# Reading the skewed bias tiles of a banded attention straight from their table, with a row step of minus one element

## The chip, the cores and the metric

The kernel runs on one core of one Trainium2 chip. The metric is the device time of one execution in microseconds (us); the median of the runs counts. A core has a matrix engine (TensorE, PE in the profile), three engines for elementwise work (VectorE or DVE, ScalarE or ACT, GpSimd or POOL) and a queue engine (SyncE, SP) that issues nearly all transfers here. The transfers run on 16 DMA engines.

## The reference, cut to what matters

One encoder layer over 1,024 tokens of width 1,024. After a first norm, two attentions run side by side: a dense one with low-rank queries and keys (8 heads, with rotary positions) and a banded one (16 heads, each token sees 128 to either side, with a bias by distance and a sink). Their gated sum goes through an output product, then comes a feed-forward part with a convolution, and a last norm. The change touches the bias of the banded attention:

```python
rel = c - WINDOW - a                     # column minus row, in a band of 128 query rows
in_band = jnp.abs(rel) <= WINDOW
bias = rel_bias[t5_bucket(rel)]          # one value per distance and head
s = einsum('bqhgd,bkhd->bhgqk', q_blk, k_blk) * scale + bias
s = jnp.where(valid, s, -1e30)           # then a softmax with the sink as one more column
```

The bias depends on the distance alone, so a row of the bias band is the row above it, moved by one element.

## The kernel before, in words

Products are made in three passes of a high and a low part, so TensorE has most of the work. The program is written stage by stage. A scheduler fixes each engine's order from estimated times, except for TensorE in the stages that matter here, whose order is written out by hand (`manual_schedule`). Every engine runs its own list in order, and an instruction that waits holds up all that stand behind it. This is so for SP too: its list of transfers is one queue.

**First stage** (lines 184 to 412). For each of eight row tiles i of 128 tokens: norm (`scaled`, `normed`), eight transposes into `pt`, a split into `ht_h` and `ht_l` (line 130), and the latent product into `pj` (line 262, 24 matmuls). `tile_step(i)` then writes the scaled latents to DRAM (`lat_d`, line 392) and keeps the rotary key `kr` (line 391). In between TensorE makes, per head h, the product of two up-projections: three transposes into `pw` (line 321), a copy by ScalarE into `wt` (line 323), the product `pm` (line 329), and a copy by VectorE into `wqk` (line 331), which goes to DRAM. `pj`, `pw` and `pm` share four PSUM buffers. The rotary tables are made by `rope_tables` (line 335): positions are loaded into `pos_i` (line 337; 1,024 elements of 4 bytes), cast to `pos_f` (line 339), and a chain of some fifteen VectorE steps over `ang` and `kk` leads to a sine and a cosine on ScalarE (lines 359, 360). `pos_i` uses one of the two buffers of `wt`.

**The bias.** Lines 282 to 291 make the small table `tc_d` in DRAM: 16 heads by 512 distances (`TW`), 32 KB. Lines 293 to 296 copy it out eight times, once for each pair t of heads, with 64 copies (`HQ`) of each head's row: `tb_d[t]` has 128 rows of 2 KB. Step `s1(t, 0)` of the banded stage (line 626) loads the bias tile `bt`, 128 rows by 320 columns (`BAND`), in two loads of 64 rows each (line 631). In each the row step is `TW - 1` elements, so that every row starts one element earlier in its copy.

**What follows.** The values of the banded attention and the rotated queries (lines 526 to 600) run after the first stage. `prep(i)` reads the latents back (`ltile`, line 520), transposes them, splits them into `lth` and `ltl` (two buffers each), and writes these to DRAM (`lt_d`, lines 574 and 575); the product `pjr` uses `lth`. Then `steps()` runs the banded attention, eight pairs t of eight steps n, with `bt` in two buffers; weights `raw` (line 103) are loaded, cast by ScalarE into `whi` (line 107), and reduced by GpSimd to `wlo` (line 110). The dense attention, the output product and the feed-forward part come after it.

Of the kernel before, what the change touches and what calls it, by code (L numbers as in the profile page):

```python
# [11 lines left out]
F32 = mybir.dt.float32  # L12
# [8 lines left out]
P = 128  # L21
# [3 lines left out]
KD = D // P  # L25
# [14 lines left out]
HQ = P // 2  # L40
BAND = HQ + 2 * WINDOW
# [6 lines left out]
TW = 512  # L48
# [28 lines left out]
def encoder_layer(ctx, tc, x, positions, norm1_g, w_in, q_a_norm_g, w_q_b, kv_a_norm_g, w_kv_b,  # L77
                  rel_bias, sinks, w_out, norm2_g, w_up, conv_w, conv_b, w_down, final_norm_g,
                  onehot, freq, out):
    nc = tc.nc  # L80
# [5 lines left out]
    dp = ctx.enter_context(tc.tile_pool(name="dp", bufs=1, space=bass.MemoryType.DRAM))  # L86
# [3 lines left out]
    mx_d = [dp.tile([P, 4, 2, KD, P], F32, name=f"mx_d{j}") for j in range(2)]  # L90
    mx_l = dp.tile([P, 4, 2, P], F32, name="mx_l")
    tc_d = dp.tile([H_B, TW], F32, name="tc_d")
    tb_d = {}
    lt_d = [dp.tile([P, 4, S], F32, name=f"lt_d{j}") for j in range(2)]
    qr_d = [dp.tile([P, H_A, 512], F32, name=f"qr_d{j}") for j in range(2)]
    lat_d = dp.tile([NT, P, Q_LORA + KV_LORA], F32, name="lat_d")
# [35 lines left out]
    def three(ps, terms):  # L132
        n = len(terms)
        for i, (a, b) in enumerate(terms):
            nc.tensor.matmul(ps, a, b, start=(i == 0), stop=(i == n - 1))  # L135
# [15 lines left out]
    def row(pool, src, n, name):  # L151
        t = pool.tile([P, n], F32, name=name)
        nc.sync.dma_start(t, bass.AP(src.tensor, src.offset, [[0, P], [1, n]]))
        return t
# [26 lines left out]
        ht_h.append(big([P, KD, 512], f"ht_h{j}"))  # L181
        ht_l.append(big([P, KD, 512], f"ht_l{j}"))

    # first norm, latents of the dense branch, tables
    with ExitStack() as p0:
        rp = p0.enter_context(tc.tile_pool(name="rp", bufs=1))
        ps = p0.enter_context(tc.tile_pool(name="ps0", bufs=1, space=PSUM))
# [66 lines left out]
        def latents(i, ks=range(KD)):  # L254
            if i not in pjs:
                pjs[i] = ps.tile([P, 512], F32, tag="pj", bufs=4, name="pj")
            tok = slice(i % 4 * P, (i % 4 + 1) * P)
            for k in ks:
                wh, wlo = wl[k // 2][0][:, k % 2, :], wl[k // 2][1][:, k % 2, :]
                th, tl = ht_h[i // 4][:, k, tok], ht_l[i // 4][:, k, tok]  # L260
                for j, (a, b) in enumerate(((th, wh), (th, wlo), (tl, wh))):
                    nc.tensor.matmul(pjs[i][:, :LAT], a, b, start=(k + j == 0), stop=(k == KD - 1 and j == 2))

        with tc.manual_schedule(engines={getattr(mybir.EngineType, e) for e in FIRST}):
# [13 lines left out]
            wl_lo(3, nc.vector)  # L278
            parted(1)
            latents(0, range(4, KD))  # L280
        # relative bias by distance, masked outside the window, then one copy per query row
        rb = rp.tile([33, H_B], F32, name="rb")
        nc.vector.memset(rb[32:33, :], 1.0)
        nc.sync.dma_start(rb[0:32, :], rel_bias)
# [5 lines left out]
        nc.vector.tensor_copy(tb, tp[0:H_B, :])  # L290
        nc.sync.dma_start(tc_d, tb)

        for t in range(KD):
            if t < KD:
                tb_d[t] = dp.tile([2, HQ, TW], F32, name=f"tb_d{t}")
                nc.sync.dma_start(tb_d[t], tc_d[2 * t:2 * t + 2, None, :].broadcast_to([2, HQ, TW]))

        srow = row(rp, sinks, H_B, "srow")
        for j in range(2):
            rows = slice(j * HQ, (j + 1) * HQ)  # L300
# [3 lines left out]
        qg = row(rp, q_a_norm_g, Q_LORA, "qg")  # L304
        kg = row(rp, kv_a_norm_g, KV_LORA, "kg")

        # per head, the product of the query and key up-projections
        wqk_v = wqk_d.rearrange("k p h c -> p k h c")
        wqn = []
        wts = {}  # L310
# [20 lines left out]
            nc.vector.tensor_copy(wqk_, pm[:, :2])  # L331
            nc.sync.dma_start(wqk_v[:, :, h, :], wqk_)

        # token tables of the rotary embedding
        def rope_tables():
            pos_i = rp.tile([P, NT], I32, tag="wt", bufs=2, padded_shape=[P, 3 * P], name="pos_i")
            nc.sync.dma_start(pos_i, positions.rearrange("(t p) -> p t", p=P))
# [63 lines left out]
        for i in range(HELD, NT):  # L401
            tile_step(i)

        # taps and bias of the convolution, one column per block of channels
        cwr = rp.tile([2 * NF, 4, P], F32, name="cwr")
        for j in range(4):
            src = conv_w[j] if j < 3 else conv_b[0]
# [23 lines left out]
        three(pj, terms)  # L431
        split(pair[0], pair[1], pj)

    # window branch and gates
    with ExitStack() as pa:
        ap_ = pa.enter_context(tc.tile_pool(name="ap_", bufs=1, reuse_waits="tile"))
        ps = pa.enter_context(tc.tile_pool(name="psA", bufs=1, space=PSUM, reuse_waits="tile"))
# [73 lines left out]
                        nc.sync.dma_start(ga_d[t][:, h_ * 512:(h_ + 1) * 512], gts.pop((t, "a", h_)))  # L511
            return [project(w, hf, post) for hf in range(2)]

        # values, token-major, high and low parts side by side
        ltiles = []

        def load_lt(n):
# [108 lines left out]
        def s1(t, n):  # L626
            g = t // 2
            if n == 0:
                bt = bts[t] = ap_.tile([P, BAND], F32, tag="bt", bufs=2, name="bt")
                for j in range(2):  # L630
                    nc.sync.dma_start(bt[j * HQ:(j + 1) * HQ],
                                      bass.AP(tb_d[t].tensor, tb_d[t].offset + j * HQ * TW + P - 1,
                                              [[TW - 1, HQ], [1, BAND]]))
            bt = bts[t]
            flat = sts[t, n] = ap_.tile([P, 2 * BAND + 2], F32, tag="st", bufs=3, name="st")
            nm = cp.tile([P, 2], F32, tag="nm", bufs=4, name="nm")
            sm = cp.tile([P, 2], F32, tag="sm", bufs=4, name="sm")
            spans = []
            for e in range(2):
                q0 = (2 * n + e) * HQ  # L640
                k0, k1 = max(q0 - WINDOW, 0), min(q0 + HQ + WINDOW, S)
                a = 1 + e * BAND + k0 - q0 + WINDOW
                spans.append((k0, k1, a, a + k1 - k0, k0 - q0 + WINDOW))
            if n == 0:
                nc.gpsimd.memset(flat[:, 1 + BAND:1 + BAND + HQ], 0.0)
            if n == NT - 1:
                nc.gpsimd.memset(flat[:, 1 + BAND - HQ:1 + BAND], 0.0)
            ends = [spans[0][2] - 1, spans[1][3]]
            nc.gpsimd.tensor_copy(flat[:, ends[0]:ends[1] + 1:ends[1] - ends[0]],
                                  nsink[:, t:t + 1].broadcast_to([P, 2]))  # L650
            for e in range(2):
                k0, k1, a, b, c0 = spans[e]
                m = 2 * n + e
                sc = ps.tile([P, 512], F32, tag="sc", bufs=2, name="sc")
                q_ = qss[t, m // 8][:, m % 8].rearrange("p j q -> p (j q)")
                three(sc[:, :k1 - k0], [(q_, kws[g][0][:, k0:k1]), (q_, kws[g][1][:, k0:k1])])
                nc.vector.tensor_tensor_reduce(
                    out=flat[:, a:b], in0=sc[:, :k1 - k0], in1=bt[:, c0:c0 + k1 - k0], scale=-1.0,
                    scalar=nsink[:, t:t + 1], op0=ALU.add, op1=ALU.min, accum_out=nm[:, e:e + 1])
                ex = flat[:, a - 1:b] if e == 0 else flat[:, a:b + 1]  # L660
                nc.scalar.activation(ex, ex, AF.Exp, bias=nm[:, e:e + 1], scale=-1.0, accum_out=sm[:, e:e + 1])
            ri = cp.tile([P, 2], F32, tag="ri", bufs=4, name="ri")
            nc.vector.reciprocal(ri, sm)  # L663
            if 0 < n < NT - 1:
                pn = flat[:, 1:1 + 2 * BAND].rearrange("p (e c) -> p e c", e=2)
                nc.gpsimd.tensor_tensor(pn, pn, ri[:, :, None].broadcast_to([P, 2, BAND]), op=ALU.mult)  # L666
            else:
                for e in range(2):
                    _, _, a, b, _ = spans[e]
                    nc.gpsimd.tensor_tensor(flat[:, a:b], flat[:, a:b], ri[:, e:e + 1].broadcast_to([P, b - a]),  # L670
                                            op=ALU.mult)
# [47 lines left out]
            next(rot, None)  # L719
        drain(rot)  # L720

        # transposed weights; the halves of a key tile that a row tile doesn't see stay zero
        pths = [[ap_.tile([P, 6, P], F32R, tag=t, bufs=2, name=t) for t in ("pth", "ptl")] for _ in range(2)]
        for w in pths[0] + pths[1]:
            nc.gpsimd.memset(f32(w[HQ:, 0]), 0.0)
# [4 lines left out]
        q0_ = queries(0)  # L730
        drain(q0_[0])
        s1(0, 0)
        drain(q0_[1])
        def steps():
            for t in range(KD):
# [13 lines left out]
                for n in range(NT):  # L749
                    for stage in range(3):  # L750
                        if stage == 0:
                            if n + 1 < NT:
                                s1(t, n + 1)
                            elif t + 1 < KD:
                                s1(t + 1, 0)
                        elif stage == 1:
                            s2(t, n)
                        elif n > 0:
                            s3(t, n - 1)
                        elif t > 0:  # L760
                            s3(t - 1, NT - 1)
                        pos += 1
                        while done < math.ceil(total * pos / 24):
                            next(chain_, None)
                            done += 1
                    if n == NT - 1:
                        drain(chain_)
                    if (t, n) == (KD - 1, ABS):
                        wqk[0] = absorbing(0)
                    yield t, n  # L770
# [7 lines left out]

    ck.close()

    # dense branch
    c1 = ExitStack()
    cc1 = c1.enter_context(tc.tile_pool(name="cc1", bufs=1, reuse_waits="tile"))

# [44 lines left out]
    with ExitStack() as pb:  # L829
# [110 lines left out]
        for i in range(ni):  # L940
# [12 lines left out]
            if i in (ni - 16, ni - 14, ni - 12, ni - 7):  # L953
                j = len(wos[0])
# [13 lines left out]
        if EARLY > 2:  # L968
            out_early(2)

    # output projection, residual, second norm; the blocks of the up product's second operand
    hq = c0.enter_context(tc.tile_pool(name="hq", bufs=1, side="right", reuse_waits="tile"))
    hs = [big([P, 2, 4, 512], f"hs{j}") for j in range(4)]
    B11, B21, B22, T1, T2, T3, T4 = range(7)
# [143 lines left out]
    first = [0, 0, 1] + [0] * 5 + [1] * 6  # L1118
# [129 lines left out]
        ready += [next(todo) for _ in range(5)]  # L1248
    c1.close()

    # up projection by seven block products (Strassen's scheme in Winograd's form), convolution and gate
    with ExitStack() as pd:
        dd = pd.enter_context(tc.tile_pool(name="dd", bufs=1, reuse_waits="tile"))
        dpool["dd"] = dd
# [55 lines left out]
    c3.close()  # L1310
    c0.close()

    # down projection by the same scheme, final norm
    with ExitStack() as pe_:
        for name in ("op", "x2", "part", "raw"):
            dpool[name] = pe_.enter_context(tc.tile_pool(name="d_" + name, bufs=1, reuse_waits="tile"))
# [13 lines left out]
        halves = (slice(0, 512), slice(512, D))  # L1330
# [24 lines left out]
        for gi, group in enumerate(groups):  # L1355
# [3 lines left out]
            for bank, phase, outs in phases:  # L1359
# [8 lines left out]
                for j, tp in turns_:  # L1368
                    if up_ and j == 0:
                        banks[bank, tp] = ps.tile([P, 512], F32, tag=bank, bufs=4, name="b" + bank)  # L1370
                    a, w = opers[j]
# [57 lines left out]
```

## Time and profile before

| what | us |
|---|---|
| three runs | 1697.89, 1698.56, 1701.55 |
| median | 1698.56 |
| span of the profiled execution (first to last instruction) | 1695.9 |
| TensorE busy in that span | 1597.8 |
| VectorE, GpSimd, ScalarE busy | 1075.1, 973.2, 900.7 |

The page gives the span of the profiled execution and no other time of it; the span is 2.7 us under the median of the runs. Times inside the execution are counted from the span's start. A row of the timeline has the start, the length, the engine, the line, the operation with its output and inputs, how many instructions are merged, and in brackets the idle time of the engine ahead of it with what ended it. "SPq" rows are the queue's own instructions that issue a transfer; their length is the time until the issue was done, not until the data landed.

### The profile page before, as it was taken

To read this page: it belongs to the slowest core of one execution; us is meant where nothing else is said; L and a number is where in the kernel's file an instruction comes from. 1 tells how busy PE (TensorE), PEld (TensorE's weight loads), DVE (VectorE), ACT (ScalarE), POOL (GpSimd) and SP (SyncE) were. 2 spreads that over 40 slices of the span, in tenths; PEclk is the share of its full clock that TensorE was granted. 3 is DMA by queue.
4 is the path that set the end of the run, shared out by engine and by line. 5 is a ranking of instruction groups with operands and counts; after the bars stand their busy time and mean duration, and the time that the engine had idled before them with its cause. 6 is when DMAs were issued, how large, how long until landed. Compare 5 with 4: busy or idle time off the path is not lost. (4 is left out here: it accounts for less than half of the span.)

```text
span 1695.9 us, 21962 instructions
## 1 busy us (share of the span) xinstructions
PE 1597.8 (94%) x7714; PEld 1318.9 (78%) x7714; DVE 1075.1 (63%) x1781; ACT 900.7 (53%) x1684; POOL 973.2 (57%) x755
## 2 busy tenths in 40 slices
PE   8299999999999999999999998999999999699998
PEld 7288788878887788888887877888888888477786
DVE  7157556556556566666653386665566665999997
ACT  6124787767787565555551264444445444343345
POOL 3002344333333375656561078888989985888884
PEclk9699999999999999999999999999999999799999
DMA  7346122111210721213125943222222222714202
GB/s 252 93 142 196 38 60 60 56 59 48 63 48 21 259 100 52 67 54 134 51 87 166 317 144 97 77 88 75 87 70 84 83 87 84 301 50 136 103 11 99
DMA packets 150102, 173.81 MB, mean 102 GB/s; under 512 B 10711, under 2 KB 111879, under 8 KB 149992
## 3 DMA queue, kind: packets, MB, share of 16 engines
q1 hardware_dynamic: 147368, 163.83, 29.4%
q0 software_dynamic: 2624, 8.59, 1.5%
q8 instruction: 61, 1.00, 0.2%
q14 instruction: 49, 0.40, 0.1%
HBM read 124.64 MB, written 49.84 MB: 103 GB/s over the span
## 5 line engine op out<-in xcount | busy, mean ns | idle before, releaser
L1112 PE MATMUL bx<-hs,op 128*128 128x512 f32 x1056 | 260.2, 398 | 5.0 <-ACT cv L1299 3.4
L1112 PEld LDWEIGHTS bx<-hs,op 128*128 128x128 f32 x1056 | 200.5, 190 | 53.0 <-ACT cv L1299 3.9
L1112 PE MATMUL byz<-hs,op 128*128 128x512 f32 x792 | 196.1, 395 | 1.6 <-ACT k L1271 1.0
L860 POOL TENSOR_TENSOR p<-p,rib 128x1024 f32<-128x1024 f32 x64 | 123.2, 1936 | 111.3 <-DVE rib L859 74.3
L1112 PEld LDWEIGHTS byz<-hs,op 128*128 128x128 f32 x792 | 149.4, 189 | 36.9 <-ACT k L1271 1.4
L445 PE MATMUL pj<-ht_h,whi 128*128 128x512 f32 x416 | 169.5, 407 | 0.0
L445 PE MATMUL pj<-ht_h,wlo 128*128 128x512 f32 x416 | 164.5, 396 | 0.0
L445 PE MATMUL pj<-ht_l,whi 128*128 128x512 f32 x416 | 164.4, 395 | 0.0
L1375 PE MATMUL bx<-op,op 128*128 128x512 f32 x528 | 134.0, 413 | 19.2 <-DVE x L789 14.1
L110 POOL TENSOR_TENSOR wlo<-raw,whi 128x512 fp32r<-128x512 f32 x64 | 82.7, 1320 | 111.4 <-ACT whi L107 111.0
L786 POOL TENSOR_TENSOR op<-s,op 128x512 fp32r<-128x512 f32 x80 | 139.6, 1749 | 8.6 <-ACT op L984 8.6
L1375 PEld LDWEIGHTS bx<-op,op 128*128 128x128 f32 x528 | 105.6, 201 | 44.9 <-DVE x L789 15.4
L666 POOL TENSOR_TENSOR st<-st,ri 128x640 f32<-128x640 f32 x48 | 60.1, 1252 | 120.8 <-DVE ri L663 120.6
L129 ACT CAST pT<-pt 128x512 fp32r<-128x512 f32 x128 | 73.8, 589 | 93.7 <-PE pt L874 93.5
L130 DVE TENSOR_TENSOR pT<-pt,pT 128x512 fp32r<-128x512 f32 x128 | 86.9, 683 | 53.1 <-ACT pT L129 53.1
L130 DVE TENSOR_TENSOR ptl<-ptw,pth 64x128 fp32r<-64x128 f32 (+2 forms) x176 | 74.3, 422 | 68.8 <-ACT pth L129 66.7
L786 POOL TENSOR_TENSOR op<-wu,op 128x512 fp32r<-128x512 f32 x64 | 96.2, 1516 | 30.0 <-ACT op L984 29.7
L852 DVE TENSOR_REDUCE nmb<-sc 128x1 f32<-128x1024 f32 x64 | 78.3, 1224 | 33.9 <-PE sc L135 33.5
L1375 PE MATMUL by<-op,op 128*128 128x512 f32 x396 | 95.5, 395 | 4.2 <-DVE op L786 3.8
L1020 ACT CAST op<-p 128x512 fp32r<-128x512 f32 x88 | 50.6, 617 | 83.1 <-PE bx L1375 54.6
L135 PE MATMUL po<-pT,ct 128*128 128x512 f32 x384 | 94.6, 395 | 0.0
L135 PE MATMUL sc<-lt_h,q 128*128 128x512 f32 x224 | 93.6, 418 | 0.0
(294 smaller groups left out, 3964.8 us busy)
## 6 DMA issues: line engine op xcount, KB each, us to landing
wu<-in_w_up_dram SPq DMA_DIRECT2D x44, 512.0 KB
raw<-in_w_in_dram SPq DMA_DIRECT2D x28, 512.0 KB
act_d<-t SPq DMA_DIRECT2D x22, 512.0 KB
ra<-act_d SPq DMA_DIRECT2D x22, 512.0 KB
rw<-in_w_down_dram SPq DMA_DIRECT2D x22, 512.0 KB
mh<-mx_d SPq DMA_DIRECT2D x16, 512.0 KB
mh<-mx_d SPq DMA_DIRECT2D x12, 448.0 KB
xt<-in_x_dram SPq DMA_DIRECT2D x8, 512.0 KB
```

The source lines that it names most:

```text
L110: nc.gpsimd.tensor_tensor(lo[:, q], raw[:, q], f32(hi[:, q]), op=ALU.subtract)
L129: nc.scalar.copy(hi, src)
L130: nc.vector.tensor_tensor(lo, src, f32(hi), op=ALU.subtract)
L135: nc.tensor.matmul(ps, a, b, start=(i == 0), stop=(i == n - 1))
L445: nc.tensor.matmul(pj, a[:, k, :], b[:, k], start=(k + j == 0), stop=(k == KD - 1 and j == 2))
L666: nc.gpsimd.tensor_tensor(pn, pn, ri[:, :, None].broadcast_to([P, 2, BAND]), op=ALU.mult)
L786: eng.tensor_tensor(dst, a, b, op=ALU.subtract)
L852: nc.vector.tensor_reduce(nm, sc, axis=AX.X, op=ALU.max, negate=True)
L860: nc.gpsimd.tensor_tensor(pe, pe, ri.broadcast_to([P, S]), op=ALU.mult)
L1020: nc.scalar.copy(t[:, 0], src)
L1112: nc.tensor.matmul(bank, a[:, i, k], hs[c][:, j, k], start=(start and n == 0), stop=(n == 11), skip_group_check=not start)
L1375: nc.tensor.matmul(banks[bank, tp], l_, r_, start=(up_ and j + n == 0), stop=(j == len(group) - 1 and n == 2), skip_group_check=not up_)
```

## The change

`tb_d` and its eight copies are gone. `bt` is loaded by one transfer of 128 rows whose source is `tc_d` itself: two heads, 64 rows per head with a step of minus one element, 320 elements each.

```diff
     tc_d = dp.tile([H_B, TW], F32, name="tc_d")
-    tb_d = {}
...
-        for t in range(KD):
-            if t < KD:
-                tb_d[t] = dp.tile([2, HQ, TW], F32, name=f"tb_d{t}")
-                nc.sync.dma_start(tb_d[t], tc_d[2 * t:2 * t + 2, None, :].broadcast_to([2, HQ, TW]))
...
                 bt = bts[t] = ap_.tile([P, BAND], F32, tag="bt", bufs=2, name="bt")
-                for j in range(2):
-                    nc.sync.dma_start(bt[j * HQ:(j + 1) * HQ],
-                                      bass.AP(tb_d[t].tensor, tb_d[t].offset + j * HQ * TW + P - 1,
-                                              [[TW - 1, HQ], [1, BAND]]))
+                nc.sync.dma_start(bt, bass.AP(tc_d.tensor, tc_d.offset + 2 * t * TW + P - 1,
+                                              [[TW, 2], [-1, HQ], [1, BAND]]))
```

The other lines of the diff are comments taken out. Since the scheduler fixes the orders anew, some instructions move. Line numbers of the changed kernel are 1 to 8 lower than before.

SP's list in the first stage, before: a weight load, the eight copies, latents of tile 1, the third weight tile, the positions.

```order
L103 DMA raw_914<-in_w_in_dram 128x4x256
L296 DMA tb_d0_249<-tc_d_82 128x1x512
L296 DMA tb_d1_251<-tc_d_82 128x1x512
L296 DMA tb_d2_253<-tc_d_82 128x1x512
L296 DMA tb_d3_255<-tc_d_82 128x1x512
L296 DMA tb_d4_257<-tc_d_82 128x1x512
L296 DMA tb_d5_259<-tc_d_82 128x1x512
L296 DMA tb_d6_261<-tc_d_82 128x1x512
L296 DMA tb_d7_263<-tc_d_82 128x1x512
L392 DMA lat_d_87<-lat_375 128x384
L103 DMA raw_1436<-in_w_in_dram 128x8x128
L337 DMA pos_i_484<-in_positions_dram 128x8x1
```

The same place on SP in the changed kernel.

```order
L102 DMA raw_898<-in_w_in_dram 128x4x256
L386 DMA lat_d_87<-lat_359 128x384
L102 DMA raw_1420<-in_w_in_dram 128x8x128
L331 DMA pos_i_468<-in_positions_dram 128x8x1
L326 DMA wqk_d_88<-wqk_465 128x2x128
```

The eight copies are gone and the rest stands in its old order.

VectorE's list a little later, before: the splits of tiles 5 and 6 (`ht_l`), latents and key of tiles 2 and 3, then the cast of the positions.

```order
L130 TENSOR_TENSOR ht_l1_112<-pt_455,ht_h1_111 128x8x128
L148 RECIPROCAL rstd2_437<-rstd_435 128x1
L130 TENSOR_TENSOR ht_l1_112<-pt_563,ht_h1_111 128x8x128
L390 SCALAR_TENSOR_TENSOR lat_439<-pj_401,rstd2_437,kg_271 128x128
L391 COPY kr_105<-pj_401 128x64
L331 COPY wqk_583<-pm_580 128x256
L148 RECIPROCAL rstd2_542<-rstd_540 128x1
L148 RECIPROCAL rstd2_546<-rstd_544 128x1
L389 SCALAR_TENSOR_TENSOR lat_548<-pj_510,rstd2_542,qg_269 128x256
L390 SCALAR_TENSOR_TENSOR lat_548<-pj_510,rstd2_546,kg_271 128x128
L391 COPY kr_105<-pj_510 128x64
L339 CAST pos_f_486<-pos_i_484 128x8
```

The same place on VectorE in the changed kernel.

```order
L333 CAST pos_f_470<-pos_i_468 128x8
L129 TENSOR_TENSOR ht_l1_112<-pt_439,ht_h1_111 128x8x128
L147 RECIPROCAL rstd2_421<-rstd_419 128x1
L338 TENSOR_TENSOR ang_474<-pos_f_470,frow_472 128x256
L129 TENSOR_TENSOR ht_l1_112<-pt_547,ht_h1_111 128x8x128
L384 SCALAR_TENSOR_TENSOR lat_423<-pj_385,rstd2_421,kg_255 128x128
L385 COPY kr_105<-pj_385 128x64
L341 TENSOR_SCALAR kk_476<-ang_474 128x256
L342 TENSOR_SCALAR kk_476<-kk_476 128x256
L344 TENSOR_SCALAR kh__479<-kk_476 128x256
L325 COPY wqk_567<-pm_564 128x256
```

The cast of the positions now stands ahead of the split of tile 5, and steps of the angle chain stand between the rest. On ScalarE the sine now stands ahead of the `wt` copy of head 4, and sine and cosine are parted by a square root, which makes two table loads more.

SP's list where the first bias tiles are loaded, before: latents read back (`ltile`), the two loads of bias tile 0, two more `ltile`, four writes of `lth` and `ltl`, the two loads of bias tile 1.

```order
L520 DMA ltile<-lat_d 128x384 x3
L631 DMA bt<-tb_d_249 64x320 x2
L520 DMA ltile<-lat_d 128x384 x2
L574 DMA lt_d_83<-lth 512x1x128
L575 DMA lt_d_84<-ltl 512x1x128
L574 DMA lt_d_83<-lth 512x1x128
L575 DMA lt_d_84<-ltl 512x1x128
L631 DMA bt<-tb_d_251 64x320 x2
L520 DMA ltile<-lat_d 128x384
```

The same place on SP in the changed kernel.

```order
L514 DMA ltile<-lat_d 128x384 x3
L624 DMA bt<-tc_d 128x1x320 x2
L514 DMA ltile<-lat_d 128x384 x2
L568 DMA lt_d_83<-lth 512x1x128
L569 DMA lt_d_84<-ltl 512x1x128
L568 DMA lt_d_83<-lth 512x1x128
L569 DMA lt_d_84<-ltl 512x1x128
L514 DMA ltile<-lat_d 128x384
```

Bias tiles 0 and 1 are now loaded by one transfer each, one behind the other, ahead of two `ltile` loads and the four writes. The six later bias tiles keep their places in the list.

## Rows read from the trace of the kernel before

**Rows 1.** The page: busy tenths of TensorE in 40 slices of the span.
```profile
PE   8299999999999999999999998999999999699998
```

**Rows 2.** Busy time by stretch: us, engines' busy us (instructions), PEclk, DMA share, GB/s.
```profile
51.50:80.70 29.20, 0.19 (x2) 0.00 (x0) 1.05 (x4) 1.46 (x3) 0.34 (x1) 0.58 0.29 85
80.70:94.70 14.00, 10.84 (x48) 9.81 (x49) 8.52 (x22) 5.33 (x17) 2.17 (x2) 0.66 0.42 131
94.70:171.00 76.30, 75.33 (x460) 66.38 (x459) 51.12 (x110) 30.45 (x62) 15.11 (x23) 1.00 0.61 176
```

**Rows 3.** Waits from 20 to 120 us: us in total, times, longest.
```profile
ACT whi L107 <- DMA raw<-in_w_in_dram: 32.9, 2, 32.5
```

**Rows 4.** Timeline of TensorE around its idle stretch: start, us, what.
```profile
45.53 0.49 PE L321 MATMUL pw<-ident,wqn 128*128 128x128 f32 x3
...
46.23 0.45 PE L262 MATMUL pj<-wlhi,ht_h 128*128 128x448 f32 x1
...
51.20 0.49 PE L321 MATMUL pw<-ident,wqn 128*128 128x128 f32 x3
80.73 1.21 PE L329 MATMUL pm<-wt 128*128 128x128 f32 x4 [29.04 <-ACT wt L323]
...
86.57 0.74 PE L262 MATMUL pj<-wlhi,ht_h 128*128 128x448 f32 x1 [3.13 <-DVE wqk L331]
...
93.19 0.49 PE L321 MATMUL pw<-ident,wqn 128*128 128x128 f32 x3
93.51 0.61 PE L329 MATMUL pm<-wt 128*128 128x128 f32 x4
...
94.75 0.45 PE L262 MATMUL pj<-wlhi,ht_h 128*128 128x448 f32 x1
```

**Rows 5.** Timeline of SP's queue: the copies and the positions.
```profile
32.45 31.09 SPq L296 DMA_DIRECT2D tb_d<-tc_d  x8
...
69.23 3.49 SPq L337 DMA_DIRECT2D pos_i<-in_positions_dram  x1
```

**Rows 6.** Copies (issue ns min/median/max), a stretch while they run, another queue's landing.
```profile
L296 SPq DMA_DIRECT2D tb_d<-tc_d x8: 617/5002/7202, 32.4 to 58.5; - x8
...
52.00:63.50 11.50, 0.00 (x0) 0.00 (x0) 0.00 (x0) 0.00 (x0) 0.00 (x0) 0.67 0.13 51
...
mx_d<-gat POOLq DMA_DIRECT2D x15, 256.0 KB, 2.7
```

**Rows 7.** Timeline of TensorE and VectorE around the positions.
```profile
38.54 0.61 PE L329 MATMUL pm<-wt 128*128 128x128 f32 x4
...
40.08 1.23 DVE L130 TENSOR_TENSOR ht_l<-pt,ht_h 128x1024 fp32r<-128x1024 f32 x1
...
42.67 0.21 DVE L391 COPY kr<-pj 128x64 f32<-128x64 f32 x1
...
79.62 0.17 DVE L339 CAST pos_f<-pos_i 128x8 f32<-128x8 int32 x1 [33.30 <-DMA pos_i<-in_positions_dram]
...
83.05 0.29 DVE L348 TENSOR_SCALAR kk<-kk 128x256 f32<-128x256 f32 x1
```

**Rows 8.** Timeline of ScalarE: a table load and the sine.
```profile
83.11 1.28 ACT L359 ACT_TABLE_LOAD   x1
88.65 0.42 ACT L359 ACTIVATE sinv<-ang 128x256 f32<-128x256 f32 x1 [4.25 <-DVE ang L356]
```

**Rows 9.** Bias loads (issue ns, first and last start us), and timeline of what stands near.
```profile
L631 SPq DMA_DIRECT2D bt<-tb_d x16: 450/588/1534, 110.1 to 470.4; - x16
...
112.48 0.59 SPq L574 DMA_DIRECT2D lt_d<-lth  x1
...
116.61 0.59 ACT L129 CAST lth<-ptq 128x512 fp32r<-128x512 f32 x1 [1.44 <-PE ptq L547]
...
119.70 0.40 PE L135 MATMUL pjr<-whi,lth 128*128 128x512 f32 x1
```

**Rows 10.** DMA packets by size from 470 to 476 us, where one bias tile is loaded.
```profile
DMA packets 235, 0.32 MB, mean 53 GB/s; under 512 B 32, under 2 KB 160, under 8 KB 235
```

## The prediction

> **What bounds the kernel now.** I read the page's slices first: TensorE is at nine tenths or more nearly everywhere, except the second slice (42 to 85 us), where it stands at two [rows 1]. The busy times by stretch show that this is one hole: from 51.5 to 80.7 us TensorE is busy 0.19 of 29.20 us, and VectorE, ScalarE and GpSimd together under 3 us, so nobody computes. Behind it, from 80.7 to 94.7, the granted clock is still 0.66, and from 94.7 on TensorE is busy 99% of the time at 1.00 [rows 2]. So TensorE sets the pace after the hole, and whatever shortens the hole moves all that follows.
>
> Who ends the hole is read backwards. The product `pm` waits 29.04 us for the copy `wt` on ScalarE [rows 4]. ScalarE itself waits 32.5 us for a weight tile [rows 3], and the same copy needs the buffer of the positions, whose cast on VectorE waits 33.30 us for `pos_i` [rows 7]. Both transfers come from SP, and SP's queue shows why they are late: the eight copies hold it from 32.45 for 31.09 us, and `pos_i` is issued at 69.23 only [rows 5]. An issue of a copy takes 5.00 us in the middle of the row, with the DMA engines busy 0.13 of their time, which is two of sixteen [rows 6]: 128 rows of 2 KB go through two engines, the queue is full, and SP stands.
>
> **The change part by part.**
>
> *Copies removed.* What the hole costs in all is TensorE's time from 51.52 (the last `pw` at 51.20 with 0.32 for its three) to the next latent product but one at 94.75, less the work done in it at full clock. That work is pm, pw, pm (1.24 us, as from 93.51 to 94.75), 24 latent matmuls (4.97, as from 46.23 to 51.20) and pw, pm, pw, pm (1.56, as from 93.19 to 94.75) [rows 4], together 7.8. 94.75 - 51.52 - 7.8 = 35.4 us: 29.04 of waiting, 3.13 for a `wqk` copy behind the angle chain [rows 4], and the rest at the lower clock [rows 2]. All of it is on the path.
>
> *What is late next.* The weight tile is no longer held and its transfer has ten idle us ahead of its reader, at no cost. `pos_i` cannot go before the first `pm` frees its buffer, at 39.15 (38.54 and 0.61, [rows 7]). How long it takes with empty queues no row shows. The bounds are 2.7 us, the landing of a larger transfer from another queue [rows 6], and 10.4 us, from issue to cast in this trace (69.23 to 79.62, [rows 5, 7]). The upper one had the copies' rows ahead of it; its issue alone took 3.49 us [rows 5]. I take 3.8: it lands at 43.0, between 41.9 and 49.6.
>
> *VectorE's order.* The cast of the positions now stands ahead of the split at 40.08, so VectorE stands from 40.0 to 43.0 and everything behind it waits too. The key of tile 2 was done 2.8 us after 40.08 (42.67 and 0.21); with the cast and one angle step among them it is done 3.6 us after the landing, at 46.6 [rows 7]. TensorE's `pw` at 45.53 [rows 4] needs the PSUM buffer that this key frees. Then three angle steps of 0.29 [rows 7] and the `wqk` copy come ahead of the latent product, which was at 46.23 [rows 4] and comes at 48.1: 1.9 us lost. Next, the sine stands on ScalarE ahead of the `wt` copy of head 4. The chain from cast to sine took 9.0 us (79.62 to 88.65, [rows 7, 8]); with three us of other VectorE work now woven in it ends near 55, and the `pm` that waits behind it loses 2.0. Two more table loads of 1.28 [rows 8] delay the next key by some 2.6 on ScalarE, of which TensorE sees 0.5, since 24 latent matmuls cover the rest. Sum 4.4, with 1 as the lower bound (an early landing) and 11 as the upper (6.6 more for a landing at 49.6). No gap in this sum is over 2 us, and I count the clock at 1.00.
>
> *New loads.* A bias tile is now one load with two as its leading count, like the copies. Its price is bounded by nothing (the loads of before took a median of 0.588 us to issue and delayed nobody, [rows 9]) and by the copies' 5.00 us per 64 rows on each of two engines [rows 6]. The copies are the nearer row, since their source has the same shape; by bytes, 1,280 of 2,048, it is 3.1 us a tile. Tiles 0 and 1 go together, so two engines are held for 6.2 to 10.0 us, and behind them on those engines stand two `ltile` and the writes of `lth`. In times of before: first load issued at 110.1, data moving some 1.2 later, the pair gone at 117.5 to 121.3, the first write of `lth` (issued 112.48) landed some 1.9 later, at 119.4 to 123.2. ScalarE's next cast into that buffer, at 116.61 before, waits for it, and TensorE's `pjr` at 119.70 needs that cast with its 0.59 [rows 9]. So TensorE waits 0.3 to 4.1 us. I take 2.0. The six later tiles are issued one per pair of heads, some 51 us apart (110.1 to 470.4 for eight tiles, [rows 9]), a whole pair ahead of their reader; that period covers 3 to 5 us, and no cost is counted.
>
> The rule that bears on this is in the Trainium skill, "DMA: Bandwidth & Descriptors", section "Why a DMA increments its semaphore by 16 and not by 1": a transfer uses the largest number of engines up to 16 that divides the slowest dimension of both its sides. It speaks against the change: by it the new loads use two engines, as the copies did (the trace agrees there, 0.13 of 16), where the old loads of 64 rows used 16. By the rule the sum stays as it is; without it, with the loads spread, the 2.0 falls away.
>
> *Rest.* In the dense stage twelve transposes and a few VectorE and ScalarE steps change places, and I allow 2 us either way.
>
> **Sum.** 35.4 - 4.4 - 2.0 = 29.0 us. The span of the profiled execution, 1695.9, becomes 1666.9. The median of the runs lies 2.7 above that span; I keep this distance: 1698.56 - 29.0 = 1669.6.
>
> **The rivals.**
> *The positions stay late.* If 1,024 single elements need 10.4 us even with empty queues, VectorE stands till 49.6 and another 6.6 us goes: 1676. For it: the only row of this transfer says so. Against it: two engines were then full of copies.
> *The new loads are spread over 16 engines* and hold nobody: 1667.6. For it: the destination has 128 rows. Against it: the copies had 128 rows too.
> *No change.* The hole could belong to the weight tile's transfer itself, being short of DMA engines, and then the copies' going moves nothing: 1698.6. Against it: a DMA share of 0.13 in the hole.
> *Slower.* The minus one could break each row into its 320 elements. `pos_i` spent 3.49 us on 1,024 elements [rows 5], so a tile of 40,960 would take at least 140 us on all engines, against a period of 51. Each of the six later tiles would come some 89 late, and the first two some 220: over 2400 in all. It decides once a tile takes over 51 us. Against it: in the old loads, whose row step of 511 is no row length either, rows went whole: 160 less 32 packets, 128, are between 512 B and 2 KB where one tile is loaded [rows 10]. The step within a row is unchanged.
>
> **How the numbers follow.** Forecast 1669.6, own range 1664.5 to 1674.5: 0.72. Positions late, 1676: 0.11. Loads spread, 1667.6: 0.10. No change: 0.04. Slower: 0.03. The range of 1664 to 1677 takes in the first three and the 2 us of the dense stage on the far side; together they hold 0.93 before the doubt in my hand-made order of events, which I put at one in eight. 0.2% is 3.4 us, about what a measurement tells from no change; the first three cases are all faster by more: faster 0.93, same 0.04, slower 0.03.
>
> **What would show it.** Right: no TensorE gap over 3 us from 40 to 66 us, granted clock 1.00 there; `pos_f` starting at 42 to 44; the latent product of 94.75 at 63 to 64; a wait of 0 to 4 us of `lth` on `lt_d` near 86. Wrong: `pos_f` near 50; a DMA share of 0.13 for longer than 10 us after the first bias loads; a wait on `bt` by VectorE; or an unmoved hole.

## The result

The changed kernel takes 1669.61 us (median of four runs, 1668.45 to 1670.66) against 1699.34 for the kernel before, a ratio of 0.9829 with a 95% interval of 0.9812 to 0.9845: 29.7 us faster, where 29.0 were forecast. The execution whose profile follows took 1670.18 us, its span is 1668.4, 27.5 us under the span of the profiled execution before.

The page of the changed kernel, TensorE's busy tenths and its granted clock in 40 slices of the span, against [rows 1]:

```profile
PE   8999999999998999999999989999999999699998
PEclk9999999999999999999999999999999999799999
```

The slice that stood at two is at nine, and the slices behind it differ little. The stretches that held the hole, in the columns of [rows 2]:

```profile
36.00:66.00 30.00, 28.37 (x173) 26.04 (x172) 18.91 (x52) 19.51 (x46) 5.28 (x4) 1.00 0.41 114
66.00:100.00 34.00, 31.41 (x216) 28.69 (x215) 20.43 (x53) 9.49 (x27) 2.50 (x7) 1.00 0.51 153
```

TensorE is busy 28.4 of the 30 us up to 66 and keeps full clock, 1.00. Its timeline there, which answers to [rows 4], has one wait of more than a microsecond:

```profile
46.40 0.61 PE L323 MATMUL pm<-wt 128*128 128x128 f32 x4
47.08 0.47 PE L261 MATMUL pj<-wlhi,ht_h 128*128 128x448 f32 x1
...
54.89 0.71 PE L323 MATMUL pm<-wt 128*128 128x128 f32 x4 [1.56 <-ACT wt L317]
...
62.03 0.45 PE L261 MATMUL pj<-wlhi,ht_h 128*128 128x448 f32 x1
```

The last row is the latent product that stood at 94.75 before: 32.7 us earlier. SP's queue (against [rows 5]) and the cast of the positions on VectorE (against [rows 7]) show why:

```profile
39.77 0.38 SPq L331 DMA_DIRECT2D pos_i<-in_positions_dram  x1
```
```profile
41.98 0.36 DVE L333 CAST pos_f<-pos_i 128x8 f32<-128x8 int32 x1 [1.43 <-DMA pos_i<-in_positions_dram]
```

The positions are issued at 39.77 instead of 69.23, the issue takes 0.38 us instead of 3.49, and 2.2 us after its start they have landed.

What the change costs stands some 27 us further on, where the first two bias tiles are loaded. The waits from 66 to 100 us, the row of the cast that waits, and TensorE's product behind it (against the last two rows of [rows 9], where the cast waited 1.44 us for `ptq` and the product for nothing):

```profile
ACT lth L128 <- DMA lt_d<-lth: 6.2, 1, 6.2
```
```profile
88.60 0.59 ACT L128 CAST lth<-ptq 128x512 fp32r<-128x512 f32 x1 [6.22 <-DMA lt_d<-lth]
```
```profile
89.24 0.50 PE L134 MATMUL pjr<-whi,lth 128*128 128x512 f32 x1 [2.16 <-ACT lth L128]
```

The buffer of `lth` is free only once its write to `lt_d` has landed, and that write was issued behind the pair of bias loads.

To see what the whole stage costs, and not that one wait alone, two points are used below for every kernel: the first `ptq` of the rotary stage on TensorE and the first `st` of the window branch on VectorE. In the kernel before and in the changed kernel:

```profile
108.99 0.49 PE L547 MATMUL ptq<-ident,ltile 128*128 128x128 f32 x3
171.39 0.42 DVE L657 CUSTOM_DVE_ANT_0 st<-sc,bt,nsink 128x192 f32<-128x192 f32 x1 [3.02 <-PE sc L135]
```
```profile
75.76 0.49 PE L541 MATMUL ptq<-ident,ltile 128*128 128x128 f32 x3
141.05 0.42 DVE L649 CUSTOM_DVE_ANT_0 st<-sc,bt,nsink 128x192 f32<-128x192 f32 x1 [3.01 <-PE sc L134]
```

The first point moved by 33.2 us, the second by 30.3: the stage between them grew from 62.4 to 65.3.

### The profile page after: what moved, and what is told of

Its sections match the earlier page's. It is cut to its first block, busy times and chain, and to the rows that moved or that the text cites. A ratio compares the mean times of both kernels' runs of the same rounds, so it can differ in the third digit from the quotient of the medians.

```text
span 1668.4 us, 21942 instructions
## 1 busy us (share of the span) xinstructions
PE 1595.4 (96%) x7714; PEld 1315.7 (79%) x7714; DVE 1078.1 (65%) x1781; ACT 903.0 (54%) x1686; POOL 974.8 (58%) x755
## 5 line engine op out<-in xcount | busy, mean ns | idle before, releaser
L1012 ACT CAST op<-p 128x512 fp32r<-128x512 f32 x88 | 50.6, 618 | 81.9 <-PE bx L1367 53.0
```

What stands on the lines that cost most here:

```text
L1012: nc.scalar.copy(t[:, 0], src)
```

## The experiments

The theory behind the forecast has two halves. The hole came from the copies' form, two as the leading count, which left them two of the sixteen DMA engines; and the new loads, with the same leading count, hold the write of `lth` for the same reason. Rivals: 2 MB of copies as such, or their place in SP's queue; and for the loads the minus one, or rows that overlap. All kernels were timed beside the kernel before. In the summary "stage" is the time from the first `ptq` to the first `st` of the profiled execution; "hole" is TensorE's longest wait from 36 to 100 us and what it waited for.

| kernel | median us | ratio to before (95%) | hole | first `ptq` | stage |
|---|---|---|---|---|---|
| before | 1699.34 | 1 | 29.04, `wt` | 108.99 | 62.4 |
| changed | 1669.61 | 0.9829 (0.9812 to 0.9845) | 2.16, `lth` | 75.76 | 65.3 |
| changed, again | 1669.06 | 0.9823 (0.9809 to 0.9837) | 2.25, `lth` | 74.70 | 66.9 |
| e7, copies unread | 1701.72 | 1.0016 (1.0006 to 1.0026) | 28.43, `wt` | 109.28 | 65.2 |
| e2, copies on 16 engines | 1663.08 | 0.9789 (0.9774 to 0.9804) | 0.70, `wqk` | 75.08 | 62.4 |
| e4, four copies | 1679.66 | 0.9893 (0.9868 to 0.9919) | 13.59, `wt` | 89.16 | 62.8 |
| e3, copies from GpSimd | 1670.42 | 0.9838 (0.9816 to 0.986) | 5.08, `wt` | 80.72 | 62.7 |
| e1, first pair on 16 | 1663.37 | 0.9792 (0.9772 to 0.9811) | under 0.5 | 73.62 | 62.9 |
| e10, reversed table | 1664.49 | 0.9805 (0.9781 to 0.9828) | 1.56, `wt` | 75.08 | 62.9 |
| e10, again | 1662.63 | 0.9787 (0.9774 to 0.9801) | 1.56, `wt` | 75.26 | 62.9 |
| e11, reversed, one load | 1670.13 | 0.9832 (0.9818 to 0.9845) | 2.33, `lth` | 74.94 | 67.0 |
| e5, positions early | 1673.45 | 0.9859 (0.9833 to 0.9886) | 3.49, `wt` | 82.84 | 66.7 |

### Copies kept but read by nobody (e7), and the changed kernel again

```
e7, against before:
-  two loads of 64 rows from tb_d[t], step TW - 1
+  nc.sync.dma_start(bt, bass.AP(tc_d.tensor, tc_d.offset + 2 * t * TW + P - 1,
+                                [[TW, 2], [-1, HQ], [1, BAND]]))
```

> The kernel before with the copies still written as they were, but read by nobody: the bias tiles come straight from the small table as in the changed kernel. Theory (the copies alone make the hole, the new loads cost some 2 us): hole of 29 us unchanged, 1699 to 1701. Rival (the loads' dependence on the copies matters too): the hole shrinks, under 1692.

> The changed kernel once more, to know what belongs to it and what to one execution. Theory (the loss of 4 to 6 us between 930 and 1010 us of the first profile belongs to that execution): the first x_d starts some 29.6 us earlier than before and the first act_d too, 1669 us or a little less. Rival (it belongs to the change): the waits of py for mh of 2 to 4 us come again and the first act_d is again only 23.6 us earlier.

The direct loads alone, with the copies still written, gain nothing and lose 3.0 us (1701.72 against 1698.74 in that series, 0.7 above the expected range). TensorE's timeline of e7 has the hole of before:

```profile
80.56 1.19 PE L329 MATMUL pm<-wt 128*128 128x128 f32 x4 [28.43 <-ACT wt L323]
```

Its stage is 65.2 us, 2.8 more than before, with a cast of `lth` that waits 6.6 us on `lt_d`. So the two parts of the change separate: dropping the copies is all of the gain, the new form of the loads a loss of some 3 us. The rival, that the loads' dependence on the copies matters, falls.

The repeated changed kernel is there for another reason. In its first profile the output projection, from the first `py` to the first `bx`, takes 84.4 us against 79.9 before, with TensorE waiting 3.5 us in all for `mh`, so that only 25.0 of the 30 us are left at its end. In the repeat that stretch takes 80.2 us and those waits 0.9. The loss of over 4 us belonged to one execution; smaller ones of this kind, waits for `mh` of 2.5 us, come in e7 and in the second profile of e10 as well.

### The copies' form (e2)

```
-  nc.sync.dma_start(tb_d[t], tc_d[2 * t:2 * t + 2, None, :].broadcast_to([2, HQ, TW]))
+  nc.sync.dma_start(bass.AP(tb_d[t].tensor, tb_d[t].offset, [[TW, HQ], [HQ * TW, 2], [1, TW]]),
+                    bass.AP(tc_d.tensor, tc_d.offset + 2 * t * TW, [[0, HQ], [TW, 2], [1, TW]]))
```

> The kernel before, with the eight copies kept and only their order of rows changed: 64 is the leading count of both sides, the bytes are the same. Theory (the hole comes from the two engines that the copies' leading count of two leaves them): eight issues in under 10 us instead of 31, the hole of 29.0 us shrinks to under 5, and since the bias loads keep their old form, lth does not wait: 1667 to 1672. Rival (2 MB of copies as such, or their place in SP's queue): the hole stays above 15 us, 1685 or more.

Same bytes, same queue, same place; only the order of the rows differs. The source row of e2 (issue time in ns, minimum, median, maximum; first and last start; landing), against the first row of [rows 6]:

```profile
L296 SPq DMA_DIRECT2D tb_d<-tc_d x8: 530/602/722, 32.4 to 37.6; - x8
...
DMA to landing us min/median/max: 5.8/6.0/6.0
```

A median of 0.60 us an issue instead of 5.00; all eight are issued within 5.7 us of time instead of 31. TensorE's longest wait up to 66 us is 0.70. At 1663.08 us the kernel with all its copies is faster than the changed kernel (0.9789, 0.9774 to 0.9804, against 0.9829, 0.9812 to 0.9845): the hole was the copies' form, not the copies. The time lies 3.9 us below the expected range.

### Half the copies (e4)

```
-            if t < KD:
+            if t < KD // 2:
                 (copy of tile t)
+  tiles 4 to 7: the direct load of the changed kernel
```

> The kernel before with only tiles 0 to 3 copied in the old form, through SP; tiles 4 to 7 are read straight from the table. Theory (the two engines' time for the copies' bytes is the hole): half of 2 MB at the 51 GB/s of the hole is 20 us from 33, so the copies end near 54 instead of some 74, pm comes near 57 to 62, hole 6 to 10 us, 1670 to 1675. Rival (only the holding of SP counts, and the queue takes four copies without filling): hole under 3 us, 1664. The first pair is read from copies by 64 rows, so lth does not wait.

SP's timeline of e4 shows the queue held not by the copies alone but by whatever comes behind them:

```profile
32.56 10.08 SPq L296 DMA_DIRECT2D tb_d<-tc_d  x4
42.74 4.92 SPq L392 DMA_DIRECT2D lat_d<-lat  x1
47.76 0.46 SPq L103 DMA_DIRECT2D raw<-in_w_in_dram  x1
48.33 4.85 SPq L337 DMA_DIRECT2D pos_i<-in_positions_dram  x1
```

The positions are cast at 58.4, ten us after their issue began, and the `pm` behind them starts at 59.87, within the 57 to 62 expected. The wait before it, though, is 13.59 us and not 6 to 10, because TensorE ran out of work at 46.3, not at 51.2 as in the kernel before: the latent products of the next tile, which it had done ahead of the hole there, now come behind it. The time, 1679.66, lies 4.7 us above the expected range. What the theory priced is where the hole ends: that `pm` starts 20.9 us earlier than before (59.87 for 80.73), where half of the bytes at 51 GB/s make 20. The rival, that only an unfilled queue counts, falls. That the wait, too, is about half of 29.04 hangs on the other order of TensorE and shows nothing by itself.

### The copies from another queue (e3)

```
-  nc.sync.dma_start(tb_d[t], ...)
+  nc.gpsimd.dma_start(tb_d[t], ...)
```

> The kernel before, with the eight copies unchanged in form but issued on GpSimd's queue instead of SP's. Theory A (the hole is SP's queue held by full queues): pos_i issues near 40 us, pos_f under 50, hole under 5 us, 1664 to 1670. Theory B (the backlog on two of the engines holds every transfer that also uses these two): pos_i issues near 40 but lands after 60, hole over 15 us, 1680 to 1699.

This was meant to separate a held SP from two engines with a backlog. It did not, because in GpSimd's queue the same copies do not stay on two engines. The DMA queues from 33 to 52 us in e3 (packets, MB, share of 16 engines' time), and below it in the kernel before:

```profile
q0 software_dynamic: 4224, 2.13, 45.9%
```
```profile
q1 hardware_dynamic: 1084, 1.57, 23.3%
```

In the kernel before SP's queue carries the copies and all else, with what runs up to 36 us among it. In e3 GpSimd's queue carries the copies alone; it takes 45.9% of the sixteen engines' time, where two engines would be 12.5% at most, and moves the 2.13 MB in packets of 504 bytes on average. SP is free, and the positions are issued at 39.30, as theory A says; but they share the engines with all these packets and land 11.1 us later:

```profile
50.39 0.17 DVE L339 CAST pos_f<-pos_i 128x8 f32<-128x8 int32 x1 [7.19 <-DMA pos_i<-in_positions_dram]
```

TensorE waits 5.08 us for it. Each theory gets a part: an issue that is not held is worth most of the hole, and a landing behind other traffic costs some 5 us.

### The first pair of bias tiles (e1)

```
         nc.sync.dma_start(tc_d, tb)
+        for t in range(2):
+            (copy of tile t, in the form of e2)
...
-  direct load
+  if t in tb_d: two loads of 64 rows from the copy, as before
+  else: direct load
```

> The changed kernel, but bias tiles 0 and 1 come from copies of theirs as before, written and read with 64 as the leading count; tiles 2 to 7 stay direct. Theory (the pair of direct loads goes through two engines and holds the first lth write): the cast of lth waits under 0.5 us on lt_d instead of 6.2, pjr no longer waits 2.2 for it, about 2 us less than the changed kernel, 1667.4. Rival (lth is late for another reason, SP's order of issues): the 6.2 and the 2.2 stay, 1669.6.

No wait of `lth` on `lt_d` is left, and the stage is 62.9 us. The time is 1663.37, 4 us lower than expected: 1.6 us of that is the wait of `pm` for `wt`, which e1 also doesn't have (its cast of the positions, at 42.01, waits 0.26 us and stands in another order of steps), and 1.5 us is the stage, which costs more than the wait that I had priced. The rest, some 1 us, is not accounted for; single runs of e1 spread from 1659.39 to 1667.47.

### Sign or leading count (e10, e11)

```
-    return rows                                   (host, the one-hot rows of the table)
+    return np.ascontiguousarray(rows[:, ::-1])
e10: two loads a tile, tc_d[2 * t + j] at TW - P - BAND + 1, [[1, HQ], [1, BAND]]
e11: one load a tile, the same offset, [[TW, 2], [1, HQ], [1, BAND]]
both: in1=bt[:, BAND - c0 - n:BAND - c0][:, ::-1]   (n columns, read backwards)
```

> The changed kernel with the small table stored in reversed order (the one-hot rows are reversed on the host), so that the rows' step becomes plus one; a tile is two loads of 64 rows with 64 as the leading count, straight from the table, and VectorE reads the tile's columns backwards. No copies. Theory (the pair costs what it costs because it goes through two engines): lth waits under 0.5 us on lt_d, first st comes 62 to 63 us after the first ptq instead of 65 to 67, 1665 to 1666. Rival (rows of 1,280 bytes that start 4 bytes apart are slow to read, whatever the engines): the wait and 65 to 67 us stay, 1669. If reading backwards costs VectorE time, the 128 tensor_tensor_reduce of the window take longer than in the changed kernel and eat the gain.

> The kernel with the reversed table, rows a step of plus one apart, but a tile is one load of 128 rows again, with two as its leading count. Theory (two engines, by the leading count; neither the sign of the row's step nor the overlap of the rows matters): the wait of lth on lt_d near 6 us and that of pjr near 2.2 are back, first st 65 to 67 us after the first ptq, 1668 to 1670. Rival (the minus one makes the old pair slow): no wait, 62 to 63 us, 1664 to 1665, as with the two loads of 64 rows.

> The kernel with the reversed table and two loads of 64 rows once more, beside the one above. Theory: 62 to 63 us from the first ptq to the first st, 1664 to 1665, some 4 to 5 us less than the one above, of which 3.4 lie between these two points. Rival (its gain was one execution's): within 1 us of the one above.

These two test the second half of the theory. Both read the same overlapping rows by a step of plus one; in the program they differ in the leading count alone, 64 or 2. In e11 the wait is back, on ScalarE and on TensorE:

```profile
87.90 0.58 ACT L128 CAST lth<-ptq 128x512 fp32r<-128x512 f32 x1 [6.38 <-DMA lt_d<-lth]
```
```profile
88.54 0.50 PE L134 MATMUL pjr<-whi,lth 128*128 128x512 f32 x1 [2.33 <-ACT lth L128]
```

In e10 there is none, and its loads land in 2.5 to 3.4 us:

```profile
L625 SPq DMA_DIRECT2D bt<-tc_d x16: 450/588/1497, 76.7 to 437.2; - x16
...
DMA to landing us min/median/max: 2.5/2.7/3.4
```

So the wait comes with the leading count of two, whatever the sign of the step, and the overlap alone does not bring it. One thing more differs, though: the scheduler puts the load of tile 1 behind the four writes in e10 and e1, as in the kernel before, and ahead of them in e11, as in the changed kernel. The wait by itself does not tell two engines from two tiles ahead of the writes. A tile that is loaded alone does. The DMA engines' busy tenths in 40 slices of 0.14 us around the load of the fifth tile, in e11 from 282 to 287.5 us, with the stretch while it runs in the columns of [rows 2], and in e10 from 276.5 to 282:

```profile
DMA  0000000000001111111111111111111111111000
284.00:286.50 2.50, 2.50 (x16) 2.20 (x16) 1.85 (x5) 2.46 (x4) 2.34 (x5) 1.00 0.13 50
```
```profile
DMA  0000000000003434453441000000000000000000
```

The same 0.16 MB take 3.4 us at 0.13 of the engines' time, two of sixteen, and 1.4 us at three to five tenths. The changed kernel's fifth tile, with the step of minus one, takes 3.4 us at 0.13 as well. So the leading count sets the number of engines and the sign does not. By these figures two tiles ahead of the writes hold the two engines for 6.8 us, and in e10 the second tile there would have added some 1.4 us (an estimate; no run has that order). What the overlap costs is small: a load of 64 rows lands in 2.7 us (median) in e10 and in 2.3 in e2, whose rows are copies, and nothing waits for it.

Busy time from 84 to 92 us (columns of [rows 2]) in e10, in the changed kernel again, and in e11:

```profile
84.00:92.00 8.00, 8.00 (x63) 7.59 (x62) 6.56 (x15) 2.78 (x6) 0.00 (x0) 1.00 0.62 177
```
```profile
84.00:92.00 8.00, 5.75 (x35) 5.17 (x34) 3.41 (x6) 1.91 (x4) 0.00 (x0) 0.84 0.59 178
```
```profile
84.00:92.00 8.00, 5.67 (x35) 5.19 (x35) 3.64 (x7) 1.91 (x4) 0.00 (x0) 0.85 0.59 180
```

e10 does 63 matmuls there, the other two 35: 2.3 us of waiting, and then a granted clock that is between its levels of 1.2 and 2.4 GHz on average (0.84, 0.85) where e10 keeps 1.00. In the repeat of the changed kernel it stands at 0.50, the lower level, from 90 to 92 us. In the first profile of the changed kernel and in e7 the clock stayed at 1.00 behind the same wait.

Reading the tile backwards costs VectorE nothing. The 96 full-width instructions of the window branch, in the changed kernel and in e10, both 548 ns:

```profile
L649 DVE CUSTOM_DVE_ANT_0 st<-sc,bt,nsink 128x320 f32<-128x320 f32 x96 | 49.4, 548 | 5.4 <-PE sc L134 4.1
```
```profile
L651 DVE CUSTOM_DVE_ANT_0 st<-sc,bt,nsink 128x320 f32<-128x320 f32 x96 | 49.4, 548 | 4.2 <-PE sc L134 2.9
```

With medians of 1664.49 and 1662.63 us, e10 is a version without copies that beats both kernels: 0.9805 and 0.9787 of the kernel before. The first series' interval just overlaps the changed kernel's (0.9781 to 0.9828 against 0.9812 to 0.9845), the second's (0.9774 to 0.9801) does not. With e1 and e2 it cannot be told apart.

### The positions in a buffer of their own (e5)

```
-  rope_tables(): pos_i in the ring of wt, loaded there
+  pos_i in a buffer of its own, loaded ahead of the bias table
```

> The changed kernel with the positions in a buffer of their own, loaded ahead of the bias table. Theory (pos_i's landing is what makes pm wait 1.56 us for wt): pos_f no longer waits, the 1.56 goes, 1667 to 1668. Rival (the order of steps on ScalarE makes the wait): within 0.5 us of the changed kernel.

It lost 4 us against the changed kernel, and neither side had that. The buffer was also what kept the angle chain back. Without it the scheduler puts the chain among the norms of the first tiles, and ScalarE switches tables four times there, from 38 us on (its timeline):

```profile
38.14 1.28 ACT L354 ACT_TABLE_LOAD   x1
39.43 0.42 ACT L354 ACTIVATE sinv<-ang 128x256 f32<-128x256 f32 x1
39.87 1.28 ACT L145 ACT_TABLE_LOAD   x1
...
42.52 1.28 ACT L355 ACT_TABLE_LOAD   x1
...
45.06 1.28 ACT L145 ACT_TABLE_LOAD   x1
```

The `wt` copy comes late, the first `pm` waits 3.49 us and starts at 45.10 instead of 39.09, and the first `ptq` is 7.1 us behind the changed kernel's. So e5 cannot tell whether the landing makes the 1.56 us. Other traces can. ScalarE in the changed kernel, and below it in e1, where the positions are cast at the same time (42.01 for 41.98):

```profile
52.76 1.28 ACT L353 ACT_TABLE_LOAD   x1
54.06 0.42 ACT L353 ACTIVATE sinv<-ang 128x256 f32<-128x256 f32 x1
54.38 0.46 ACT L317 COPY wt<-pw 128x384 f32<-128x384 f32 x1
```
```profile
52.14 0.47 ACT L322 COPY wt<-pw 128x384 f32<-128x384 f32 x1
...
53.08 1.28 ACT L358 ACT_TABLE_LOAD   x1
```

In the changed kernel the copy `wt` stands behind the table load and the sine, and the sine does not wait for the end of the angle chain; in e1 the copy stands ahead of both, and `pm` does not wait. The same order as in the changed kernel brings the same 1.56 us in its repeat, in e10 twice and in e11. So the order of steps on ScalarE makes the wait, as the rival said, and not the landing.

## Why the prediction was right

**The hole.** It was read rightly: who ends it, why both transfers are late, and what it costs. The latent product moved by 32.7 us, where the working gave 35.4 - 4.4 = 31.0. The 4.4 were too high by 1.7. Step by step: the positions took 2.2 us to land, below even the lower bound of 2.7, which came from a transfer 64 times as large; the upper bound of 10.4 was traffic and nothing of the transfer's own (10.1 in e4 and 11.1 in e3, both behind copies). The latent product expected at 48.1 came at 47.08, and since this execution was already 0.55 us behind at the first `pm` (39.09 for 38.54), only 0.3 of the 1.9 was lost. The wait for `wt` behind the sine was 1.56 for 2.0. The granted clock is 1.00 there.

**The bias loads.** Place and mechanism were as forecast: `lth` waits 6.22 us on `lt_d`, `pjr` 2.16 of 2.0 expected. The mis-sized term is what that wait costs. I priced the wait with the clock at 1.00, and stopped. The stage between the two points takes 65.2 to 67.0 us in the five profiles with a pair on two engines (the changed kernel twice, e5, e7, e11) and 62.4 to 62.9 in the seven without; means 66.2 and 62.7, so 3.5 us. The price of a tile itself was right: 3.4 us measured, between the 3.1 and 5.0 of the working. The five fall into two kinds by the granted clock behind the wait: 65.2 and 65.3 where it stays at 1.00 (e7 and the first profile of the changed kernel), 66.7 to 67.0 where it falls to some 0.85 (the other three). So the wait costs 2.5 us at full clock, and 1.6 us more where the clock falls.

The rule of the Trainium skill, "DMA: Bandwidth & Descriptors", section "Why a DMA increments its semaphore by 16 and not by 1", that the slowest dimension's count sets the number of engines, is what e2, e10 and e11 turn on, and on SP's queue their traces agree with it (5.00 and 0.60 us an issue for the same bytes; 3.4 us at 0.13 of the engines or 1.4 at three to five tenths for one tile). On GpSimd's queue e3 shows more than two engines for a leading count of two, 45.9% of sixteen. The same section names an exception there, by which some direct copies from GpSimd go over sixteen engines.

**The sum.** Two errors of about equal size work against each other: 1.7 us more gained in the hole, 1.5 more lost at the loads. A second pair does so at the end. The span was forecast at 1666.9 and measured at 1668.4 (1667.8 in the repeat), and the median lies 1.2 us above it (1.3 in the repeat), where the prediction kept the 2.7 of before. That the time came out within 0.1 us of 1669.6 is luck; that it came out within a few is the mechanism.

**The signs named beforehand.** No wait of TensorE up to 66 us is over 1.56 us, the clock is 1.00, and `pos_f` starts at 41.98, at the edge of 42 to 44. Two signs missed: the latent product came at 62.03, ahead of 63 to 64, and `lth` waited 6.22 us, not 0 to 4. The second did not fit the prediction's own working, whose 0.3 to 4.1 us are the wait of `pjr`; ScalarE, idle from 115.2 there with a write that lands at 119.4 or later [rows 9], had to wait over 4.

**The rivals.** Positions that stay late: ruled out by the 2.2 us. Loads spread over sixteen engines: ruled out by the wait, and by e10 and e1, which show what spreading is worth, 3.5 us in the stage instead of the 2.0 I gave it. No change: ruled out by the time itself, and by e2 and e4. Rows broken into elements: a tile that loads alone takes 3.4 us, not 140, and VectorE never waits for `bt`.

**What the prediction didn't ask.** It took the copies' removal for the cure. e2 shows that the kernel before needed only another order of the same rows, and the change carries the copies' fault over into the loads.

**What stays open.** The medians of the kernels with the pair on two engines and no hole (1669.6, 1669.1, 1670.1) and those without it (1663.4, 1663.1, 1664.5, 1662.6) lie 6.2 us apart, of which the stage explains 3.5 and the first `ptq` 0.4; their profiled spans lie 4.9 apart. In the series of e11 and the repeat of e10 the medians lie 7.5 apart where 4 to 5 were expected, with 4.1 in the stage. The output projection takes 81.9 us on average in the former's profiles and 80.3 in the latter's, but single ones run from 80.2 to 84.4 and from 79.6 to 81.9, so whether the loads have a part in that is not settled.

## What to carry to other kernels

When a queue stands and the DMA share is a small multiple of a sixteenth, look at the leading count of the transfer before its bytes: the same copies with their rows in another order gave 35.7 us here, and one load cut into two whose leading count is 64 gave 5.1 and 7.5 us over the kernels with one load. A wait on the engine that sets the pace is to be priced with what stands behind it, the clock too: 2.2 to 2.5 us of wait came to 2.5 us at full clock and to 4.2 where the clock fell. A buffer that makes a step wait may be what holds a scheduler's order together; moving it moves more than the wait.

## What the runs showed of the hardware that was not expected

- 128 rows of eight single integers each land 2.2 us after the start of their issue when nothing holds SP's queue and the DMA engines are at 0.40 of their time, less than the 2.7 us of a 256 KB transfer.
- Copies with a leading count of two are spread over the engines when GpSimd issues them: 4224 packets of 504 bytes on average, 45.9% of the engines' time, each of the eight landing in 9.0 to 11.7 us, where SP's queue was held for 31.
- One load of 128 rows of 1,280 bytes takes 3.4 us alone with a leading count of two, whether the rows' step is plus or minus one, and 1.4 us as two loads of 64 rows.
- A VectorE instruction that reads one operand backwards takes the same 548 ns.
- Behind the wait of `pjr` at the same place the granted clock over the stretch was 0.84 to 0.86 in three executions and 1.00 in two; the stage was 1.6 us longer in the three.
